# State space stage of a hybrid decoder: where tap loads queue, how many projection banks, how far apart the groups

## The chip, the cores and the metric

The kernel runs on one core of one Trainium2 chip. The metric is the device time of one execution in microseconds; the median of three runs of the kernel before is 1704.26 us. Engine names are those of the profile: PE is TensorE's matrix multiply and PEld its weight load, DVE is VectorE, ACT is ScalarE, POOL is GpSimd, SP is the engine that issues all DMAs here.

## The reference, cut

Two layers on a (1024, 1024) float32 sequence. Layer 0 is dilated attention. Layer 1, where the change lies, is a state space layer:

```python
def s5_mixer(h, w_in, ..., w_glu, b_glu, w_out):
    proj = h @ w_in                                   # 1024 x 2048
    u, z = proj[..., :SSM_WIDTH], proj[..., SSM_WIDTH:]
    y = s5_scan(u, ...)        # 64 groups of 16 channels, 64 complex states each
    g = jax.nn.gelu(y)
    y = g * jax.nn.sigmoid(g @ w_glu + b_glu)
    return (y * jax.nn.silu(z)) @ w_out

# in s5_scan, per group:
#   states_t = a_bar * states_(t-1) + b_bar u_t ;  y_t = Re(C states_t) + d u_t
```

Both layers are wrapped in RMS norms and a residual addition. Float32 products are made on TensorE from a high and a low part of each operand, three matmuls per product (high·high, high·low, low·high).

## The kernel before, in words

The sequence is cut in halves of 512 tokens. A *half projection* is 24 matmuls (8 slices of the inner dimension, three products each) of one 128-column block `e` of the weight with one token half `th`, into one bank of PSUM. The input projection of layer 1 has 16 blocks, so 32 halves, counted t = 0 to 31: blocks 0 to 7 give u, 8 to 15 give z. `in_order` emits them; `proj_half` takes the bank from the pool `psj`, which has two. `use_u` copies a bank with ScalarE (L1389) and stores it to DRAM (`u_dr`, L1391); `use_z` forms silu with ScalarE (L1396) and VectorE (L1397) and stores it (`z_dr`, L1398). A bank is free for the next half when its last reader is through. Each block's weight is loaded (L95), split in high (`whi`, ScalarE, L83) and low part (`wlo`, VectorE, L84).

The scan is cut in eight groups of SSM heads, one object `Ssm` each, with five stages:

- `ssm_loads`: tables from DRAM: BT, Cg, Sg, and CA (576 KB), two buffers each.
- `ssm_taps`: eight DMAs of 64 KB bring the short convolution M ("taps"). Taps of groups 0 to 3 share one large tile (tag `b1`), those of 4 to 7 another (`b3`).
- `ssm_input`: reads the group's u back in another layout, as U (512 KB), two buffers.
- `ssm_states`: matmuls pv = BT·U (L1339), rotation by Cg and Sg and scans on VectorE, two multiplies or additions on GpSimd, result X (L1352).
- `ssm_outputs`: matmuls py = M·U + CA·X (L1366, L1367), GELU over ScalarE, GpSimd and VectorE (L1368 to L1373), store to `y_dr` (L1374).

`layer1` writes down after which half t each stage of each group is emitted: group e begins at 3e, its loads at +3 (earlier for groups 0 and 1), taps at +4, U at +5, states at +7, outputs at +10. That order is a priority. The final order on each engine is found at build time by a scheduler that plays the program through with a cost model and takes, on each engine, the first instruction in priority that is ready at that moment of its model; `high_priority` moves work ahead by 600 places. On the chip each engine then works through its list strictly in order, waiting on semaphores. `tc.issue_after(x)` puts what is traced in its block behind `x` in the list of `x`'s engine, with no wait for `x` to finish.

After the stage comes `glu`: it reads y back (`gy`, L1431), splits it in high and low part (g0 in the tiles `b1` and `b3`, which held the taps; g1 in `b4`, `b5`), and starts with four half projections at once in two `psj` and two `psl` banks (`psb`), seven of the eight inner slices first, the eighth at the end.

PSUM has eight banks in four pools of two here: `psj` (projections), `pst` (transposes, of the norm before the stage), `pso` (py) and `psl` (pv).

Of the kernel before, what the change touches and what calls it, by code (L numbers as in the profile page):

```python
# [15 lines left out]
F32 = mybir.dt.float32  # L16
# [7 lines left out]
P = 128  # L24
# [3 lines left out]
H = 512  # L28
# [61 lines left out]
def load_w(c, src):  # L90

    nc = c.nc
    with c.tc.high_priority(AHEAD):
        raw = c.wraw.tile([P, KT * P], F32, tag="wraw", name="wraw")
        nc.sync.dma_start(raw, src)  # L95
        hi = c.wsp.tile([P, KT * P], F32R, tag="whi", name="whi")
        lo = c.wsp.tile([P, KT * P], F32R, tag="wlo", name="wlo")
        c.last_lo = split(c, hi, lo, raw, engine=c.w_engine).ins
    return hi, lo


def proj_part(c, ps, w, h, ks, first=True):

    nc = c.nc
    wh, wl = w
    hh, hl = h
    for k in ks:
        s = slice(k * P, k * P + P)
        for n, (a, b) in enumerate(((wh, hh), (wh, hl), (wl, hh))):
            nc.tensor.matmul(ps, a[:, s], b[:, k, :], start=first and k == 0 and n == 0,  # L110
                             stop=k == KT - 1 and n == 2, skip_group_check=True)


def proj_half(c, w, h):

    ps = c.psj.tile([P, H], F32, tag="psj", name="psj")
    proj_part(c, ps, w, h, range(KT))
    return ps

# [629 lines left out]
def in_order(c, srcs, h, use, after=None, start=None, ws=()):  # L749

    t = 0

    def one(e, th, ps):
        nonlocal t
        use(e, th, ps)
        if after:
            after(t)
        t += 1  # L760

    ws = list(ws) or [load_w(c, srcs[e]) for e in range(2 if start else 0)]
    if start == "block":
        jobs = [(e, th) + ((c.psj, "psj"), (c.psl, "psl"))[th] for th in range(2) for e in range(2)]
        pss = [pool.tile([P, H], F32, tag=tag, name="psb") for _, _, pool, tag in jobs]
        for ks in (range(KT - 1), (KT - 1,)):
            for ps, (e, th, _, _) in zip(pss, jobs):
                proj_part(c, ps, ws[e], h[th], ks)
                if ks[0]:
                    one(e, th, ps)  # L770
    elif start == "half":
        for e in range(2):
            one(e, 0, proj_half(c, ws[e], h[0]))
        pss = [c.psj.tile([P, H], F32, tag="psj", name="psj") for _ in range(2)]
        for part in range(2):
            cs = slice(part * 256, part * 256 + 256)
            for e in range(2):
                proj_part(c, pss[e][:, cs], ws[e], [x[:, :, cs] for x in h[1]], range(KT), part == 0)
                if part:
                    one(e, 1, pss[e])  # L780
    for e in range(len(ws), len(srcs)):
        w = load_w(c, srcs[e])
        for th in range(2):
            one(e, th, proj_half(c, w, h[th]))


def silu2(c, t, ps):
# [7 lines left out]
def attn_gate(c, a, h):  # L795

    nc = c.nc
    g = [(c.pb.tile([P, KT, H], F32R, tag=f"b{i}", name=f"gh{i}"),
          c.pb.tile([P, KT, H], F32R, tag=f"b{2 + i}", name=f"gl{i}")) for i in range(2)]
    raw = [c.pb.tile([P, KT, H], F32, tag=f"b{4 + i}", name=f"wo{i}") for i in range(2)]  # L800

    def load_out(p, n):
        nc.sync.dma_start(raw[n][:, p, :], a["w_out"][p, :, n * H:n * H + H])

    def early(p):
        load_out(p, 0)
        for i in range(2):
            if p == 7:
                f = c.last[:, i * H:i * H + H]
            else:  # L810
                f = c.slot("fz")
                nc.sync.dma_start(f, c.on_dr[p, :, i * H:i * H + H])
            split(c, g[i][0][:, p, :], g[i][1][:, p, :], f)

    def use(p, th, ps):
        if th == 0:
            load_out(p, 0)
        t = c.slot("tz")
        silu2(c, t, ps)
        f = c.slot("fz").rearrange("p (i n) -> p i n", i=8)  # L820
        nc.sync.dma_start(f, c.on_dr[p].rearrange("p (i n) -> p i n", i=8)[:, :, 64 * th:64 * th + 64])
        nc.gpsimd.tensor_tensor(f, f, t.rearrange("p (n i) -> p i n", i=8), op=ALU.mult)
        for i in range(2):
            dh, dl = (x[:, p, :].rearrange("p (i n) -> p i n", i=4)[:, :, 64 * th:64 * th + 64] for x in g[i])
            split(c, dh, dl, f[:, 4 * i:4 * i + 4, :])

    def step(t):
        if t < 7 - EARLY:
            early(EARLY + t)

    in_order(c, [a["w_in"][48 + p] for p in range(EARLY)], h, use, step)
    run_merge(c)
    early(7)
    for p in range(8):
        load_out(p, 1)
    return g, raw
# [453 lines left out]
def ssm_loads(self):  # L1290

    c, et = self.c, self.et
    nc = c.nc

    def tl(name, w=128):
        return c.ssm.tile([P, 8, w], F32, name=name, tag=name, bufs=2)

    self.BT, self.Cg, self.Sg = tl("BT"), tl("Cg"), tl("Sg")
    self.CA = tl("CA", 144)
    dr = c.rot_dr  # L1300
    nc.sync.dma_start(self.BT, c.bt_dr[et].rearrange("p (g x) -> p g x", g=8))
    for hf in HEADS:
        nc.sync.dma_start(self.Cg[hf].rearrange("p g x -> p (g x)"),
                          bass.AP(dr.tensor, dr.offset + et * 3 * 64 * S, [[S, 64], [1, S]]))
    nc.sync.dma_start(self.Sg.rearrange("p g x -> p (g x)"),
                      bass.AP(dr.tensor, dr.offset + (et * 3 + 1) * 64 * S, [[S, P], [1, S]]))
    nc.sync.dma_start(self.CA, c.ca_dr[et].rearrange("p (g x) -> p g x", g=8))


def ssm_taps(self):  # L1310

    c, et = self.c, self.et
    if et % 4 == 0:
        c.taps.append(c.pb.tile([P, 4, 8, P], F32, tag=("b1", "b3")[et // 4], name="taps"))
    t = self.M = c.taps[et // 4][:, et % 4]
    for m in range(8):
        src = bass.AP(c.k_dr.tensor, c.k_dr.offset + et * 8 * 16 * 240 + 16 * m, [[240, 16], [16 * 240, 8], [1, 128]])
        c.nc.sync.dma_start(t[16 * m:16 * m + 16], src)


def ssm_input(self):
    c = self.c
    self.U = c.ssm.tile([P, 8, P], F32, name="U", tag="U", bufs=2)
    c.nc.sync.dma_start(self.U, c.u_dr[self.et].rearrange("p (g n) -> p g n", g=8))


def ssm_states(self):
# [54 lines left out]
def layer1(c, a, h1, ws):  # L1382

    nc, tc = c.nc, c.tc
    c.ssm = c.es_pa.enter_context(tc.tile_pool(name="ssm", bufs=1, side="left", reuse_waits="tile"))
    def use_u(et, th, ps):
        ut = c.slot("ut")
        with tc.high_priority(AHEAD):
            nc.scalar.copy(ut.rearrange("p (i n) -> p i n", i=4)[:, ::-1, :], ps.rearrange("p (i n) -> p i n", i=4))  # L1389
            dst = bass.AP(c.u_dr.tensor, c.u_dr.offset + et * P * S + (1 - th) * 4 * 16384, [[P, P], [16384, 4], [1, P]])  # L1390
            nc.sync.dma_start(dst, ut.rearrange("p (i n) -> p i n", i=4))  # L1391

    def use_z(et, th, ps):
        z = c.slot("z1")
        with tc.high_priority(AHEAD):
            nc.scalar.activation(z, ps, AF.Tanh, scale=0.5)  # L1396
            nc.vector.scalar_tensor_tensor(z, z, 1.0, ps, op0=ALU.add, op1=ALU.mult)  # L1397
            nc.sync.dma_start(c.z_dr[et, :, th * H:th * H + H], z)  # L1398

    groups = [Ssm(c, a, e) for e in range(8)]  # L1400
    c.taps = []
    at = [[] for _ in range(40)]
    for e in range(8):
        t = 3 * e
        for stage, d in ((ssm_loads, (-1, -2)[e] if e < 2 else 3), (ssm_taps, 4), (ssm_input, 5), (ssm_states, 7), (ssm_outputs, 10)):
            at[t + d + 1].append((stage, e))

    def run(t):
        for stage, e in at[t + 1]:
            stage(groups[e])  # L1410

    def use(e, th, ps):
        (use_u if e < 8 else use_z)(e % 8, th, ps)

    run(-1)
    in_order(c, [a["ssm_w_in"][e] for e in range(16)], h1, use, run, start="half", ws=ws)
    for t in range(32, 39):
        run(t)
# [32 lines left out]
def trunk(tc, a):  # L1451
    c = Ctx()
    nc = tc.nc
    c.nc, c.tc = nc, tc
    c.turn = 0
    with ExitStack() as es:
        pool = lambda name, **k: es.enter_context(tc.tile_pool(name=name, **k))
        c.cst = pool("cst", bufs=1)
# [45 lines left out]
        g, raw = attn_gate(c, a, h)  # L1504
# [112 lines left out]
```

## Time and profile before

| | |
|---|---|
| median of three runs (lowest to highest) | 1704.26 us (1700.07 to 1706.83) |
| the profiled execution's own time | 1699.39 us |
| its span, first to last instruction | 1697.6 us |
| busy in the span: PE, DVE, ACT, POOL | 98%, 60%, 42%, 27% |
| first projection matmul of layer 1 | 1261.33 us |
| last output matmul of group 7 | about 1501.8 us |
| first matmul after the four starting banks of the GLU | 1532.87 us |
| DMA share from 1261.33 to 1501.77 | 0.68, at 202 GB/s |

The profile is one execution. A row of the timeline gives start, duration, engine, line, operation, tiles (written <- read), shape and count, and in brackets how long the engine had been idle and what released it. A row of a window gives start and end, length, busy time and count by engine, the granted TensorE clock (1.00 is full), the DMA engines' mean busy share and their GB/s. Matmuls are pipelined: one of 512 columns is shown with 0.40 us, and the next starts 0.23 us after it.

### The profile page before, as it was taken

To read this page: it belongs to the slowest core of one execution; us is meant where nothing else is said; L and a number is where in the kernel's file an instruction comes from. 1 tells how busy PE (TensorE), PEld (TensorE's weight loads), DVE (VectorE), ACT (ScalarE), POOL (GpSimd) and SP (SyncE) were. 2 spreads that over 40 slices of the span, in tenths; PEclk is the share of its full clock that TensorE was granted. 3 is DMA by queue.
4 is the path that set the end of the run, shared out by engine and by line. 5 is a ranking of instruction groups with operands and counts; after the bars stand their busy time and mean duration, and the time that the engine had idled before them with its cause. 6 is when DMAs were issued, how large, how long until landed. Compare 5 with 4: busy or idle time off the path is not lost. (4 is left out here: it accounts for less than half of the span.)

```text
span 1697.6 us, 26292 instructions
## 1 busy us (share of the span) xinstructions
PE 1657.5 (98%) x9714; PEld 1397.0 (82%) x9714; DVE 1014.2 (60%) x2509; ACT 711.9 (42%) x1730; POOL 461.0 (27%) x303
## 2 busy tenths in 40 slices
PE   8999999999999999999999999999999999989998
PEld 6889999978888888888888888877887888867886
DVE  8698898625554554545454554657562787755533
ACT  5232232236465464655555454653452223233411
POOL 2000001132242525223351614213220445413121
PEclk9999999999999999999999999999999999989999
DMA  6223455532331423232242424236259865465432
GB/s 236 84 55 101 147 175 162 174 95 65 87 106 54 117 70 103 78 91 90 77 117 82 113 68 124 78 110 167 87 169 237 232 203 202 143 186 162 149 118 87
DMA packets 176857, 212.19 MB, mean 125 GB/s; under 512 B 37443, under 2 KB 133462, under 8 KB 176728
## 3 DMA queue, kind: packets, MB, share of 16 engines
q1 hardware_dynamic: 176728, 210.52, 41.5%
q8 instruction: 76, 1.25, 0.3%
q14 instruction: 53, 0.43, 0.1%
HBM read 153.51 MB, written 56.96 MB: 124 GB/s over the span
## 5 line engine op out<-in xcount | busy, mean ns | idle before, releaser
L110 PE MATMUL psj<-hh,whi 128*128 128x512 f32 x896 | 359.6, 401 | 3.7 <-DVE tz L792 3.7
L110 PE MATMUL psj<-hh,wlo 128*128 128x512 f32 x896 | 359.4, 401 | 0.0
L110 PE MATMUL psj<-hl,whi 128*128 128x512 f32 x896 | 356.4, 398 | 0.0
L84 POOL TENSOR_TENSOR wlo<-wraw,whi 128x1024 fp32r<-128x1024 f32 x48 | 115.2, 2400 | 395.4 <-ACT whi L83 365.1
L110 PEld LDWEIGHTS psj<-hh,whi 128*128 128x128 f32 x896 | 169.6, 189 | 41.2 <-DVE tz L792 4.1
L110 PEld LDWEIGHTS psj<-hh,wlo 128*128 128x128 f32 x896 | 169.4, 189 | 36.6
L110 PEld LDWEIGHTS psj<-hl,whi 128*128 128x128 f32 x896 | 169.4, 189 | 36.4
L486 ACT ACTIVATE lg<-lg,nm 128x128 f32<-128x128 f32 (+1 forms) x384 | 168.2, 442 | 37.4 <-DVE nm L481 37.4
L83 ACT CAST whi<-wraw 128x1024 fp32r<-128x1024 f32 x80 | 83.7, 1046 | 192.5 <-PE psj L110 127.1
L475 DVE CUSTOM_DVE_ANT_0 lg<-psl,T 128x128 f32<-128x128 f32 (+1 forms) x384 | 110.6, 347 | 88.6 <-PE psl L469 88.6
L371 PE MATMUL psq<-whi,v 128*128 128x256 f32 x640 | 120.3, 284 | 0.0
L110 PE MATMUL psj<-h1h,whi 128*128 128x512 f32 (+1 forms) x272 | 106.7, 393 | 8.0 <-DVE z L1397 7.8
L84 DVE TENSOR_TENSOR ph<-pt,ph 128x512 fp32r<-128x512 f32 (+2 forms) x160 | 96.8, 622 | 15.3 <-ACT ph L83 13.1
L110 PE MATMUL psj<-h1l,whi 128*128 128x512 f32 (+1 forms) x272 | 105.7, 389 | 0.1
L110 PE MATMUL psj<-h1h,wlo 128*128 128x512 f32 (+1 forms) x272 | 105.2, 388 | 0.0
L84 DVE TENSOR_TENSOR kl<-psj,kh 128x512 fp32r<-128x512 f32 x48 | 33.2, 692 | 119.8 <-ACT kh L83 119.2
L371 PEld LDWEIGHTS psq<-whi,v 128*128 128x128 f32 x640 | 100.0, 189 | 1.2 <-issue 1.2
L83 ACT CAST ph<-pt 128x512 fp32r<-128x512 f32 (+2 forms) x160 | 81.5, 529 | 46.5 <-PE pt L497 45.5
L371 PE MATMUL psq<-wlo,v 128*128 128x256 f32 x320 | 91.3, 286 | 0.5 <-DVE wlo L84 0.5
L546 PE MATMUL pso<-ph,vs 128*128 128x256 f32 (+1 forms) x544 | 86.7, 284 | 0.0
L497 PE MATMUL pt<-identr,lg 128*128 128x128 f32 x560 | 82.2, 277 | 0.0
L1213 POOL TENSOR_TENSOR Ks<-Ks,O 128x16 f32<-128x16 f32 x8 | 4.3, 534 | 284.4 <-ACT Ks L1211 284.4
(283 smaller groups left out, 3696.8 us busy)
## 6 DMA issues: line engine op xcount, KB each, us to landing
wraw<-in_w_in_dram SPq DMA_DIRECT2D x56, 512.0 KB
mw<-wt_dr SPq DMA_DIRECT2D x48, 256.0 KB
v<-in_w_v_dram SPq DMA_DIRECT2D x20, 512.0 KB
vp<-v_dr SPq DMA_DIRECT2D x16, 512.0 KB
wraw<-in_ssm_w_in_dram SPq DMA_DIRECT2D x16, 512.0 KB
v_dr<-v SPq DMA_DIRECT2D x30, 256.0 KB
rot_dr<-rt SPq DMA_DIRECT2D x48, 128.0 KB
ca_dr<-ca SPq DMA_DIRECT2D x32, 144.0 KB
```

Of the source, the lines that this page charges most:

```text
L83: nc.scalar.copy(hi, src)
L84: return (engine or nc.vector).tensor_tensor(lo, src, f32(hi), op=ALU.subtract)
L110: nc.tensor.matmul(ps, a[:, s], b[:, k, :], start=first and k == 0 and n == 0, stop=k == KT - 1 and n == 2, skip_group_check=True)
L371: nc.tensor.matmul(o, r[x][:, k, ts], w[y][:, k, :], skip_group_check=True, start=i in (0, 4, 5) and t % 2 == k == n == 0, stop=k == 3 and ...
L475: nc.vector.tensor_tensor_reduce(lg[:, h, j, 0:w], psl[:, h, o], bt[:, h, 256 - w:256], scale=1.0, scalar=-3.0e38, op0=ALU.add, op1=ALU.ma ...
L486: nc.scalar.activation(lg[:, h, j, 0:w], lg[:, h, j, 0:w], AF.Exp, bias=nm[:, h, b:b + 1], accum_out=ms[:, col:col + 1])
L497: c.nc.tensor.transpose(pt[:, n * P:(n + 1) * P], lg[:, h, j, part * P:part * P + P], c.ident)
L546: nc.tensor.matmul(o, l, r, start=n == 0, stop=n == len(jobs) - 1, skip_group_check=True)
L1213: nc.gpsimd.tensor_tensor(Ks[:, 0:16], Ks[:, 0:16], self.dd, op=ALU.add)
```

## The change

- `proj_half` takes its bank in turn from `psj` and `pst` after the opening of the stage (`c.wide`), so that projections have four banks instead of two. In the rest of the kernel `c.wide` is 0.
- CA moves from `ssm_loads` to the end of `ssm_taps`. Taps and CA of a group are issued behind the load of that group's U; `ssm_taps` moves from +4 to +6, behind `ssm_input`.
- U has three buffers.
- Group e begins at (11e + 2) // 4, that is at 0, 3, 6, 8, 11, 14, 17, 19 instead of 0, 3, 6, 9, 12, 15, 18, 21.
- The tables of group 1 are issued behind the load of U of group 0 (emitted at half 5 instead of half 1).

```diff
 def proj_half(c, w, h):
-    ps = c.psj.tile([P, H], F32, tag="psj", name="psj")
+    pool, tag = ((c.psj, "psj"), (c.pst, "pst"))[c.banks % 2]
+    c.banks += c.wide
+    ps = pool.tile([P, H], F32, tag=tag, name="psj")
     proj_part(c, ps, w, h, range(KT))
...
 def in_order(...):
+    c.wide = 1 if start == "half" else c.wide
     for e in range(len(ws), len(srcs)):
         w = load_w(c, srcs[e])
         for th in range(2):
             one(e, th, proj_half(c, w, h[th]))
+    c.banks = c.wide = 0
...
 def ssm_loads(self):
-    self.CA = tl("CA", 144)
...
-    nc.sync.dma_start(self.CA, c.ca_dr[et].rearrange("p (g x) -> p g x", g=8))
...
 def ssm_taps(self):
-    for m in range(8):
-        src = bass.AP(...)
-        c.nc.sync.dma_start(t[16 * m:16 * m + 16], src)
+    self.CA = c.ssm.tile([P, 8, 144], F32, name="CA", tag="CA", bufs=2)
+    with c.tc.issue_after(self.load_U.ins):
+        for m in range(8):
+            src = bass.AP(...)
+            c.nc.sync.dma_start(t[16 * m:16 * m + 16], src)
+        c.nc.sync.dma_start(self.CA, c.ca_dr[et].rearrange("p (g x) -> p g x", g=8))
...
 def ssm_input(self):
-    self.U = c.ssm.tile([P, 8, P], F32, name="U", tag="U", bufs=2)
-    c.nc.sync.dma_start(self.U, ...)
+    self.U = c.ssm.tile([P, 8, P], F32, name="U", tag="U", bufs=3)
+    self.load_U = c.nc.sync.dma_start(self.U, ...)
...
 def layer1(...):
     for e in range(8):
-        t = 3 * e
-        for stage, d in ((ssm_loads, (-1, -2)[e] if e < 2 else 3), (ssm_taps, 4), (ssm_input, 5), (ssm_states, 7), (ssm_outputs, 10)):
+        t = (11 * e + 2) // 4
+        for stage, d in ((ssm_loads, (-1, 2)[e] if e < 2 else 3), (ssm_input, 5), (ssm_taps, 6), (ssm_states, 7), (ssm_outputs, 10)):
             at[t + d + 1].append((stage, e))

     def run(t):
         for stage, e in at[t + 1]:
-            stage(groups[e])
+            if stage is ssm_loads and e == 1:
+                with tc.issue_after(groups[0].load_U.ins):
+                    stage(groups[e])
+            else:
+                stage(groups[e])
```

More of the change, by code (lines that the diff above doesn't have):

```diff
@@ L1315, in ssm_taps @@
     t = self.M = c.taps[et // 4][:, et % 4]
-    for m in range(8):
-        src = bass.AP(c.k_dr.tensor, c.k_dr.offset + et * 8 * 16 * 240 + 16 * m, [[240, 16], [16 * 240, 8], [1, 128]])
-        c.nc.sync.dma_start(t[16 * m:16 * m + 16], src)
+    self.CA = c.ssm.tile([P, 8, 144], F32, name="CA", tag="CA", bufs=2)
+    with c.tc.issue_after(self.load_U.ins):
+        for m in range(8):
+            src = bass.AP(c.k_dr.tensor, c.k_dr.offset + et * 8 * 16 * 240 + 16 * m, [[240, 16], [16 * 240, 8], [1, 128]])
+            c.nc.sync.dma_start(t[16 * m:16 * m + 16], src)
+        c.nc.sync.dma_start(self.CA, c.ca_dr[et].rearrange("p (g x) -> p g x", g=8))
 def ssm_input(self):
     c = self.c
-    self.U = c.ssm.tile([P, 8, P], F32, name="U", tag="U", bufs=2)
-    c.nc.sync.dma_start(self.U, c.u_dr[self.et].rearrange("p (g n) -> p g n", g=8))
+    self.U = c.ssm.tile([P, 8, P], F32, name="U", tag="U", bufs=3)
+    self.load_U = c.nc.sync.dma_start(self.U, c.u_dr[self.et].rearrange("p (g n) -> p g n", g=8))
 def ssm_states(self):
@@ L1455, in trunk @@
     c.turn = 0
+    c.banks, c.wide = 0, 0
     with ExitStack() as es:
```

## The prediction

> **What bounds the kernel now.** I read the page first, then TensorE's waits in the stretch that the change touches, then time-ordered rows around each wait, then windows for rates and clock. All windows are microseconds from the start of the span.
>
> ```profile
> PE 1657.5 (98%) x9714; PEld 1397.0 (82%) x9714; DVE 1014.2 (60%) x2509; ACT 711.9 (42%) x1730; POOL 461.0 (27%) x303
> ```
>
> TensorE has work in 98% of the span, so only two things can shorten it: idle stretches of TensorE, and stretches in which its clock is cut. The state space stage runs from the first projection matmul (1261.33) to the last output matmul of group 7 (1501.77); the gated linear unit (GLU) then opens with 96 matmuls into four banks, until 1532.87. The waits of TensorE in these two stretches (total, times, longest), and the stretches themselves (length, busy time and count of each engine, granted clock, DMA share, GB/s):
>
> ```profile
> PE psj L110 <- DVE z L1397: 7.8, 3, 3.6
> PE psb L110 <- ACT g0b L83: 3.5, 2, 2.4
> PE pv L1339 <- DMA U<-u_dr: 2.6, 1, 2.6
> ...
> 1261.33:1501.77 240.44, 229.72 (x1218) 194.26 (x1216) 160.42 (x246) 66.88 (x108) 82.75 (x78) 0.99 0.68 202
> 1502.00:1532.87 30.87, 26.50 (x97) 19.69 (x95) 17.33 (x24) 14.51 (x25) 7.63 (x6) 0.89 0.69 201
> ```
>
> So three causes: TensorE waits for VectorE to empty a projection bank (L1397), for an input U of a group, and, at the GLU's start, for the split of g. Where they stand, in TensorE's order of time (start, duration, instruction, count, idle before and its releaser):
>
> ```profile
> 1303.23 0.40 PE L110 MATMUL psj<-h1h,wlo 128*128 128x512 f32 x1
> 1306.25 0.49 PE L1339 MATMUL pv<-U,BT 128*128 128x128 f32 x2 [2.62 <-DMA U<-u_dr]
> ...
> 1397.41 0.50 PE L110 MATMUL psj<-h1h,whi 128*128 128x512 f32 x1 [2.06 <-DVE z L1397]
> ...
> 1491.46 0.59 PE L110 MATMUL psj<-h1h,whi 128*128 128x512 f32 x1 [3.62 <-DVE z L1397]
> ...
> 1501.77 1.71 PE L110 MATMUL psb<-g0b,whi 128*128 128x512 f32 x3
> ...
> 1519.27 1.22 PE L110 MATMUL psb<-g0b,whi 128*128 128x512 f32 x2 [2.40 <-ACT g0b L83]
> ...
> 1532.87 0.73 PE L110 MATMUL psj<-g0b,whi 128*128 128x512 f32 x2 [0.67 <-ACT whi L83]
> ```
>
> The wait costs more than itself. Two halves of 24 matmuls (one right after the U wait, one after the 3.62 us wait) against one in an undisturbed place, projection matmuls alone:
>
> ```profile
> 1306.49:1313.72 7.23, 7.23 (x24) 5.54 (x24) 0.00 (x0) 0.00 (x0) 0.76 0.88 168
> 1491.46:1498.72 7.26, 7.26 (x24) 5.59 (x24) 0.68 (x1) 0.00 (x0) 0.76 0.85 253
> 1397.41:1403.13 5.72, 5.71 (x24) 4.44 (x24) 0.68 (x1) 0.00 (x0) 1.00 0.79 243
> ```
>
> The granted clock is 0.76 there and the half takes 7.23 and 7.26 us instead of 5.72: 1.5 us more, each time. The 2.06 us wait left the clock at 1.00.
>
> **The change, part by part.** *Loads of taps and CA behind U (SP's queue).* No DMA is added or removed: 64 tap loads, 8 CA, 8 U. Their order changes. Before, the queue of SP (start, duration, count) and one ACT row show why U is late:
>
> ```profile
> 1285.85 1.06 ACT L1389 COPY ut<-psj 128x512 f32<-128x512 f32 x2
> ...
> 1291.29 5.42 SPq L1318 DMA_DIRECT2D taps<-k_dr  x11
> 1296.96 0.93 SPq L1391 DMA_DIRECT2D u_dr<-ut  x2
> ...
> 1300.76 0.98 SPq L1324 DMA_DIRECT2D U<-u_dr  x2
> ```
>
> The copies of u were done at 1286.9, but their stores were issued at 1296.96, behind tap loads, about 0.49 us of issue each (5.42 / 11), and U was read only at 1300.76. With every tap load (and the loads of group 1) behind U of group 0, the stores go out at once and U can be asked for some 8 to 10 us sooner; its first use then comes before no wait. I take the whole 2.6 us and the 1.5 us of cut clock: 4.1. What the moved loads cost: taps and CA of group 0 and the loads of group 1 (0.5, 0.6 and 1.5 MB) now start near 1292 and are due at group 0's outputs, three halves and a group after 1308, near 1327; 2.6 MB at the stage's mean 202 GB/s are 13 us of 35. Hidden, with other traffic beside it. The bounds are 0 and what a late weight would cost (a rival below). Later groups: taps are due four halves (22 us) after their U is asked for.
>
> *Four banks.* From half 4 on, projections alternate between two psj banks and two pst banks (pst last served the transposes, done at 1279). The wait it removes, on VectorE's side:
>
> ```profile
> 1393.38 0.60 ACT L1396 ACTIVATE z<-psj 128x512 f32<-128x512 f32 x1 [4.31 <-PE psj L110]
> ...
> 1395.54 1.23 DVE L84 TENSOR_TENSOR wlo<-wraw,whi 128x1024 fp32r<-128x1024 f32 x1 [0.20 <-DVE T L1351]
> 1396.68 0.68 DVE L1397 SCALAR_TENSOR_TENSOR z<-z,psj 128x512 f32<-128x512 f32 x1
> ```
>
> ScalarE had read the bank at 1394.0, VectorE got to z at 1396.68, behind the group's rotations and a weight split, and the next projection began at 1397.41. With two more banks VectorE may be two halves (11.4 us) later before TensorE feels it. All three waits go: 7.8, and 1.5 of cut clock. Together 9.3. No instruction is added; z's own ring of buffers is unchanged.
>
> *Three U buffers.* With the new spacing U of group 3 is asked for after half 13, the very half after which group 1 has its outputs and would free the buffer; with a third buffer it need not wait. Its cost is room only.
>
> *Groups every 2.75 halves.* Group 7 begins after half 19 instead of 21, so its outputs come after half 29 instead of 31, and two halves (11.4 us) of projections lie behind them. That bears on the GLU's start, where rows of three engines show the tail (VectorE's six g splits could not begin before taps of groups 4 to 7 were read for the last time, since both live in the same memory):
>
> ```profile
> 1502.23 5.20 DVE L84 TENSOR_TENSOR g0b<-gy,g0b 128x512 fp32r<-128x512 f32 x6
> ...
> 1511.49 0.33 SPq L1374 DMA_DIRECT2D y_dr<-Y  x1
> 1515.71 5.46 SPq L1431 DMA_DIRECT2D gy<-y_dr  x5
> ...
> 1518.60 0.62 ACT L83 CAST g0b<-gy 128x512 fp32r<-128x512 f32 x1 [5.89 <-DMA gy<-y_dr]
> ```
>
> The chain from group 7's last output to its g takes 1518.6 + 1.2 − 1501.8, about 18 us. Now 11.4 us of projections and the first 84 of the 96 GLU matmuls (84 × 0.237 = 20 us) cover it. The 96 took 31.1 us from 1501.77 to 1532.87; at 5.7 / 24 us each they need 22.8. Of the 8.3 us I take 7: the 0.67 wait for a weight at the end stays, since its buffer is freed only by these matmuls.
>
> *What is late next.* VectorE and the groups' own chain. From group 2's pv to group 7's, five groups, and a group's chain in the z half (pv read, X done), beside TensorE's three blocks:
>
> ```profile
> 1359.03:1475.30 116.27, 112.11 (x602) 94.97 (x601) 92.99 (x131) 32.52 (x53) 53.00 (x51) 1.00 0.59 194
> ...
> 1376.59 0.38 PE L1366 MATMUL py<-U,taps 128*128 128x128 f32 x2
> 1380.15 1.95 PE L1339 MATMUL pv<-U,BT 128*128 128x128 f32 x16
> 1381.86 0.48 PE L110 MATMUL psj<-h1h,whi 128*128 128x512 f32 x1
> ...
> 1381.25 0.69 DVE L1340 TENSOR_TENSOR T<-Cg,pv 128x512 f32<-128x512 f32 x1 [3.15 <-PE pv L1339]
> ...
> 1397.28 1.28 DVE L1352 TENSOR_TENSOR X<-X,T 128x508 f32<-128x508 f32 x2
> ```
>
> VectorE does 92.99 / 5 = 18.6 us a group. TensorE needs 2.75 × 5.7 + 3.56 (py) + 1.71 (pv) = 20.9 us a group, so VectorE is at 89% against 80% (92.99 / 116.27) now: still not the bound, but the two short gaps of two halves (16.7 us) are under 18.6. And X was ready 17.3 us after pv (1381.25 to 1398.56), where three halves give 17.1. An output matmul may therefore wait for X in the five groups 3 to 7. The trace shows no such wait. Bounds: 0 each (the order then puts another half in between) and the 2.06 us of the bank wait each, 10.3 in all. I take 0.8 each, 4 us, nearer the lower end, because X of the first half of a group is ready sooner.
>
> **Sum**: 4.1 + 9.3 + 7 − 4 = 16.4 us off. With the ends of the unknown part, nothing and 10.3 in place of the 4, and 1.3 more at the GLU, it lies between 10.1 and 21.7. The profiled execution took 1699.39 us (span 1697.6), 4.9 under the median 1704.26 of the three timed runs. Against it the sum gives 1683.0, against the median 1687.9; the next kernel's runs will scatter in the same way, so I forecast 1686, between the two.
>
> **The rivals.** *The last groups slip* (1694). If X is late in each z group and the order puts a half in front of each output, group 7's outputs come after half 31 as now. The stage's 13.4 us stay, less some 3 of waits, the GLU's 7 do not come: 1704.3 − 10.4 = 1694. For it: 17.3 against 17.1 us above, and the short gaps. Against it: VectorE has 2.3 us a group to spare (20.9 − 18.6) to catch up.
>
> *VectorE becomes the bound* (up to 1707). The multiply of the rotation that reads two operands from on-chip memory varies (min/median/max of 16), and GpSimd's multiply beside it shows with what:
>
> ```profile
> L1351 DVE TENSOR_TENSOR T<-Sg,T x16: 684/1171/1682, 1323.1 to 1488.7; 64x512 f32<-64x512 f32 x16
> ...
> 1391.64 1.72 POOL L1348 TENSOR_TENSOR X<-Cg,T 128x508 f32<-128x508 f32 x1 [1.01 <-DVE T L1346]
> 1392.24 1.66 DVE L1351 TENSOR_TENSOR T<-Sg,T 64x512 f32<-64x512 f32 x1
> ```
>
> The 1.66 us one began inside GpSimd's 1.72. GpSimd is busy 53.00 / 5 = 10.6 us a group, which will fall into 20.9 us instead of 23.3, so more of the eight such operations of a group (L1350, L1351, L1352 and L1373, twice) can meet it. At 1.0 us each (1682 − 684) for the seven not already hit, a group takes 25.6 us, 4.7 over TensorE's 20.9; in the five groups from 3 on that is 23.5 us, more than the 20.4 gained: 1707. It decides from 2.3 us a group on. Against it: the mean over five groups holds such meetings already, and VectorE's and GpSimd's order within a group does not change. [...]
>
> *Taps late at every group* (slower, 1716). The nine loads of a group sit behind its U in a queue that goes in order. From asking for U to CA's landing I estimate 9 × 0.49 us of issue and 1.1 MB at 202 GB/s, together 10 us, against 22 us until the outputs. From 22 us on, each further microsecond is paid eight times; at 26 us it is 32 us, so 1704.3 − 20.4 + 32 = 1716. For it: from 1306 to 1313 the DMA engines were 0.88 busy while they moved only 168 GB/s, so the taps' small packets are dear, and they now come when weights, U, tables and stores all want the engines. Against it: the stage as a whole is at 0.68 and no byte is added; the loads that now wait were those that crowded 1261 to 1306.
>
> *It does not do what it says* (1704). The order on SP is fixed at build time, and the banks might be freed by the same late VectorE. But an order behind U is an order, and three half projections of slack stand where there was one.
>
> [...]
>
> **How the numbers follow.** The forecast 0.61; the last groups slip 0.18; VectorE bound 0.09; taps late 0.08; nothing happens 0.04. A measurement of this kernel can tell about 0.5% (8.5 us) from no change, so faster means under 1695.8. That holds the forecast, and most of the slip case (0.14): 0.75. Within 0.5%: 0.04 of the slip case, VectorE bound, nothing: 0.17. Slower: 0.08. The range 1676 to 1700: below by 4.9 for the scatter of runs under the lower end of the sum against the median (1704.3 − 21.7 = 1682.6) with 1.7 to spare; above over the slip case and half of the VectorE one. It leaves out about 0.17. The forecast's own range is 1678 to 1693.
>
> **What would show each step.** Right: no wait of pv for U, and stores of u issued within 2 us of their copies; no wait of psj or pst matmuls for L1397; the stage's TensorE clock at 1.00 throughout; the last py before the last two halves; the 96 GLU matmuls in under 25 us. Wrong: waits of py (L1366, L1367) for X L1352, for taps or CA; weights cast late (whi waiting for wraw, with TensorE waiting behind); VectorE above 19.5 us a group; py of group 7 again directly ahead of psb; clock cuts in the new places.

## The result, and the profile after

The changed kernel takes 1692.66 us (median of five runs, 1690.53 to 1694.92), the kernel before 1704.25 us (1700.07 to 1706.83): a ratio of 0.9932, 95% interval 0.9919 to 0.9944, or 11.6 us less. The profiled execution took 1692.66 us with a span of 1690.9. The forecast was 1686 in a range of 1676 to 1700. Ratios leave out executions at a lower clock; there is one in all that follows, of `gyo_before` (2011.59 us at a granted clock of 0.75, which its median includes).

The largest waits of TensorE in the state space stage and in the opening of the GLU, 1255 to 1545 us of the changed kernel (waiting line and its releaser: total, times, longest):

```profile
PE py L1372 <- DVE X L1357: 3.1, 1, 3.1
PE psb L110 <- ACT whi L83: 1.7, 1, 1.7
PE psb L110 <- ACT g0b L83: 1.4, 2, 1.2
PE py L1372 <- POOL Y L1376: 1.1, 1, 1.1
...
```

The wait for U and all waits for z (now L1402) are gone. Two waits of py came, in the blocks of groups 4 and 7, and the GLU's matmuls (psb) still wait. Next, windows of the changed kernel: the stage from its first projection to the first GLU matmul, the opening of the GLU, eight microseconds of that opening, and the py block of group 4 (length, busy time and count by engine, granted clock, DMA share, GB/s):

```profile
1261.90:1493.82 231.92, 227.40 (x1218) 193.05 (x1216) 163.84 (x247) 67.04 (x110) 85.34 (x82) 0.99 0.72 209
1493.82:1525.37 31.55, 27.55 (x97) 19.91 (x97) 15.57 (x23) 14.27 (x23) 3.15 (x3) 0.84 0.71 210
...
1496.97:1505.00 8.03, 6.16 (x12) 3.63 (x13) 5.86 (x8) 4.04 (x7) 0.00 (x0) 0.50 0.93 279
...
1411.37:1419.91 8.54, 5.43 (x34) 5.24 (x33) 6.13 (x9) 2.59 (x4) 0.59 (x2) 0.80 0.91 260
```

Stage and opening together take 263.5 us. Before they took 271.5 (1261.33 to 1532.87), so 8.1 us of the gain lie here, and they lie in the stage: 231.9 against 240.4. The opening kept its length (31.55 us; 1501.77 to 1532.87 was 31.1). The profiled spans differ by 6.7 us (1697.6 and 1690.9) where the medians differ by 11.6: the profiled execution before was 4.9 us under its median.

The chain of SyncE around U of group 0, the changed kernel (start, duration, instruction, count):

```profile
1287.01 0.36 SPq L1396 DMA_DIRECT2D u_dr<-ut  x1
...
1288.45 0.36 SPq L1396 DMA_DIRECT2D u_dr<-ut  x1
1289.35 0.33 SPq L1329 DMA_DIRECT2D U<-u_dr  x1
...
1309.48 1.95 PE L1344 MATMUL pv<-U,BT 128*128 128x128 f32 x16
```

U is asked for at 1289.35 instead of 1300.76, 20 us ahead of pv, which starts with no wait.

The last group did move: its py block (1477.37, with the wait of 1.1) ends at 1482.14, and two half projections lie between it and the GLU. Yet the opening is as long as before, and it is still matmuls that wait for g0, g1 and a weight that set it (start, duration, instruction, count, idle before and its releaser):

```profile
1496.97 1.22 PE L110 MATMUL psb<-g0b,whi 128*128 128x512 f32 x2 [1.69 <-ACT whi L83]
1499.67 1.22 PE L110 MATMUL psb<-g1b,whi 128*128 128x512 f32 x2 [0.65 <-ACT g1b L83]
1502.08 1.22 PE L110 MATMUL psb<-g0b,whi 128*128 128x512 f32 x2 [1.18 <-ACT g0b L83]
```

### The profile page after: what moved, and what is told of

The parts are those of the page before. It is cut to its first block, busy times and chain, and to the rows that moved or that the text cites. A ratio compares the mean times of both kernels' runs of the same rounds, so it can differ in the third digit from the quotient of the medians.

```text
span 1690.9 us, 26326 instructions
## 1 busy us (share of the span) xinstructions
PE 1654.9 (98%) x9714; PEld 1394.5 (82%) x9714; DVE 1016.6 (60%) x2509; ACT 711.9 (42%) x1730; POOL 456.1 (27%) x303
## 3 DMA queue, kind: packets, MB, share of 16 engines
q8 instruction: 76, 1.25, 0.3%
## 4 chain that ended last, share of the span: by engine, by line
PE 89%; DVE 5%; DMA 4%; issue 1%; SPq 1%; ACT 0%; POOL 0%; DVEq 0%; ACTq 0%; POOLq 0%
PE psj L110 47%; PE psq L373 11%; PE psl L471 5%; PE pso L548 4%; PE pt L499 4%; PE pso L852 4%; PE pso L851 3%; PE pso L850 3%; PE psb L110 1%; PE pso L574 1%; PE psv L234 1%; PE psv L232 1%; PE psv L233 1%; PE pst L127 1%; DVE T L1351 1%
```

## The experiments

Times are medians, and each ratio is against the kernel before, run beside it. "Opening" is the time from the first GLU matmul to the first matmul after the 96.

| run | us (ratio) | 95% interval | opening, us |
|---|---|---|---|
| changed kernel | 1692.66 (0.9932) | 0.9919 to 0.9944 | 31.6 |
| `banks` | 1690.68 (0.9930) | 0.9914 to 0.9945 | 34.4 |
| `order` | 1696.52 (0.9962) | 0.9948 to 0.9977 | 29.9 |
| `sp3` | 1689.26 (0.9920) | 0.9904 to 0.9937 | 33.6 |
| `gyo` | 1691.99 (0.9941) | 0.9921 to 0.9960 | 24.5 |
| `y1o` | 1686.57 (0.9901) | 0.9883 to 0.9918 | 31.6 |
| `gyo_y1o` | 1679.37 (0.9851) | 0.9828 to 0.9874 | 23.5 |
| `sp3_gyo` | 1677.52 (0.9845) | 0.9827 to 0.9862 | 23.4 |
| `sp3f_gyo` | 1680.40 (0.9863) | 0.9844 to 0.9881 | 23.0 |
| `space` | 1702.83 (1.0005) | 0.9993 to 1.0017 | 31.3 |
| `nobanks` | 1698.55 (0.9980) | 0.9969 to 0.9992 | 30.2 |
| `gyo_before` | 1698.65 (0.9977) | 0.9966 to 0.9989 | 24.0 |
| `banks_gyo` | 1678.98 (0.9875) | 0.9860 to 0.9889 | 23.4 |

**`banks`: the kernel before with four banks alone.**

```diff
-    ps = c.psj.tile([P, H], F32, tag="psj", name="psj")
+    pool, tag = ((c.psj, "psj"), (c.pst, "pst"))[c.banks % 2]
+    c.banks += c.wide
```

> The kernel before with the four projection banks and nothing else of the change. If the waits for L1397 were a matter of banks, all three go (7.8 us, and the half speed half behind the longest, 1.5): 1704.3 becomes about 1695, the U wait of 2.6 stays, and the GLU's 96 opening matmuls keep their 31 us. If VectorE was the bound behind the banks, the waits come back in another place (an output matmul waiting for X, or a half later the same wait) and the time stays above 1700.

1690.68 us, 12.4 less than the kernel before beside it. In the traces the stage is 12.4 us shorter (228.0, from 1261.97 to 1489.99) and the opening 3.3 longer. Its largest waits of TensorE, 1255 to 1545 us:

```profile
PE psb L110 <- DVE g0b L84: 2.8, 2, 2.2
PE psb L110 <- ACT whi L83: 2.3, 1, 2.3
PE psj L110 <- ACT whi L83: 2.3, 2, 1.6
PE psb L110 <- ACT g0b L83: 0.8, 2, 0.5
...
```

The timeline has pv of group 0 at:

```profile
1311.44 2.05 PE L1343 MATMUL pv<-U,BT 128*128 128x128 f32 x16
```

The z waits are gone, and so is the wait of pv for U, though no load was moved. The reason is in the order: pv now stands behind eight full halves (it starts at 1311.44), where it stood behind seven before (1306.25, after its wait). That with two banks the eighth half had no free bank at that point of the build-time order, and pv was put ahead of it for that reason, is inferred; that four banks move pv by one half and end the wait is shown. The U wait had two sufficient cures.

**`order`: the order of the loads alone** (two banks, two U buffers, a group every three halves).

```diff
-    c.banks += c.wide
+    c.banks += 0
...
-    self.U = c.ssm.tile([P, 8, P], F32, name="U", tag="U", bufs=3)
+    self.U = c.ssm.tile([P, 8, P], F32, name="U", tag="U", bufs=2)
...
-        t = (11 * e + 2) // 4
+        t = 3 * e
```

> The kernel before with the order of loads alone: taps and CA behind U, the tables of group 1 behind U of group 0; groups every 3 halves, two banks, two U buffers. If the crowd of tap loads made U late, the U wait (2.6) and the half speed half behind it (1.5) go, and 1704.3 becomes about 1700. If the moved loads come late somewhere else (a weight, a store of y, tables), the gain is eaten and new waits stand in the z halves: 1702 to 1708.

1696.52 us, 6.5 less; in the traces the stage is 4.2 us shorter (236.3), which is the 4.1 of the prediction, and the opening 1.2 shorter. No wait for U, with pv still behind seven halves; the z waits, in the waits of TensorE, stay as they were:

```profile
PE psj L110 <- DVE z L1402: 7.7, 3, 3.6
```

**`sp3`: the whole change, but a group every three halves.**

```diff
-        t = (11 * e + 2) // 4
+        t = 3 * e
```

> The changed kernel with groups every 3 halves instead of 2.75; all else as changed. Theory: the wait of group 4's outputs for X (3 us and half speed behind it, 8.5 us for a block of 3.6) comes from the gap of two halves between groups 2 and 3; at 3 halves it goes, and the GLU's opening matmuls do not care, since they wait for reads of y that are queued behind the last two z: 1692.7 becomes about 1687. Rival: group 7's outputs behind the last half make the GLU wait for y longer, as forecast, and 2.75 is worth its wait: 1693 to 1699.

1689.26 us, 13.8 less. There is no wait of py left, and stage and opening take 259.8 us (1263.45 to 1523.22). The intervals of this run and of the changed kernel overlap, so the times alone don't rank the two; the traces show 263.5 against 259.8 us and the two py waits in one only. The 2.75 spacing costs the stage 5.7 us there (231.9 against 226.2) and shortens the opening by 2.0 (31.6 against 33.6). That `banks` (12.4) and `order` (6.5) sum to more than 13.8 fits the shared cure of the U wait.

**`gyo`: the changed kernel with buffers of its own for gy.** If the opening waits for group 7's data, this changes nothing; if it waits for the buffers that gy is read into, the opening shortens. The buffers are four tiles of a pool that lies idle in the stage, two reads to a tile, instead of the ring of seven slots (tags a and b, taken in turn) that z also uses.

```diff
-            y = c.slot("gy")
+            if et % 2 == 0:
+                yo = c.outs.tile([P, D], F32, tag="O", name="gy", bufs=4)
+            y = yo[:, et % 2 * H:et % 2 * H + H]
```

> The changed kernel with the reads of y for the GLU (gy) in buffers of their own (four tiles of two reads each, in a pool that is idle then) instead of the ring that they share with z. Theory: the GLU's gain did not come because gy, in the ring, gets its buffers behind z of halves 30 and 31 and its even blocks before its odd ones; with own buffers the 96 opening matmuls take 23 to 25 us instead of 31.5, and 1692.7 becomes about 1686. Rival 1: the splits on VectorE and ScalarE or the DMA rate are the bound: under 2 us are gained. Rival 2: early reads crowd VectorE's and ScalarE's queues in the z halves, and waits for X grow: 1693 or more.

The opening fell by 7.0, to 24.5 us at a full clock. The groups of gy's reads, first of the changed kernel, then of `gyo` (count: min/median/max ns, first and last start):

```profile
L1440 SPq DMA_DIRECT2D gy<-y_dr x16: 359/366/547, 1489.9 to 1512.8; - x16
```

```profile
L1442 SPq DMA_DIRECT2D gy<-y_dr x16: 359/371/565, 1343.6 to 1505.1; - x16
```

and the window of `gyo`'s opening:

```profile
1497.42:1521.93 24.51, 22.90 (x97) 17.83 (x95) 11.16 (x18) 9.12 (x15) 2.58 (x2) 1.00 0.69 215
```

In the changed kernel not one of the 16 reads starts before 1489.9; the first of `gyo`, at 1343.6, shows how early the first groups lie in DRAM. And the last seven start after the last z store, long after the store of group 7 (1486.66); SyncE's rows of the changed kernel (start, duration, instruction, count):

```profile
1486.66 2.86 SPq L1379 DMA_DIRECT2D y_dr<-Y  x2
1489.87 1.53 SPq L1440 DMA_DIRECT2D gy<-y_dr  x3
1491.45 0.50 SPq L1403 DMA_DIRECT2D z_dr<-z  x1
1494.52 3.97 SPq L1440 DMA_DIRECT2D gy<-y_dr  x6
1499.11 0.43 SPq L1403 DMA_DIRECT2D z_dr<-z  x1
1499.64 0.52 SPq L1440 DMA_DIRECT2D gy<-y_dr  x1
...
1502.78 10.36 SPq L1440 DMA_DIRECT2D gy<-y_dr  x6
```

and the waits of SyncE's queue from 1486 to 1515 us (total, times, longest):

```profile
SPq L1440 <- DVE g0b L84: 7.2, 6, 1.4
SPq L1379 <- DVE Y L1378: 5.5, 2, 3.4
...
SPq L1440 <- DMA z_dr<-z: 1.0, 1, 1.0
```

The reads wait for the split of an earlier gy and for the store of a z, that is for a slot of the ring. In SyncE's list as built they also stand behind the two stores of group 7's y, for which SyncE waited 5.5 us: three reads ahead of the store of z of half 30, six between it and that of half 31 (blocks 1 and 3 of the first token half behind the even ones), the other seven behind both. With buffers of their own, 13 of the 16 reads stand ahead of these stores, six of them far up in the stage. The buffers decide both the waits for slots on the chip and the order that the scheduler finds, for reads and for matmuls; the run does not separate the two.

The time is 1691.99 us all the same, for the two py waits and their cut clocks grew (0.69 from 1411 to 1422; blocks of groups 4 and 7: 9.90 and 7.43 us, where an undisturbed one takes 3.57 and the changed kernel had 8.54 and 4.77); TensorE's waits in `gyo`:

```profile
PE py L1372 <- DVE X L1357: 3.2, 1, 3.2
PE py L1372 <- POOL Y L1376: 2.1, 1, 2.1
```

So 7 us were won in the opening and 3.7 of them paid in the stage (235.6 against 231.9). The rest of the loss is not in this trace, whose execution took 1688.47 us, the shortest of the six. What made the py blocks longer here wasn't isolated.

**`y1o`: the changed kernel with more buffers for y (Y1).** Its theory: the wait of py for X of group 4 comes from the output of group 3, which has no buffer to be written to, because group 2's stores are late. Y1 had two buffers (`bufs=2`), not the four of the expectation below.

```diff
-        T1, T2 = (c.ssm.tile([P, 4, P], F32, name=n, tag=n, bufs=2) for n in ("Y1", "Y2"))
+        if b == 0:
+            yo = c.outs.tile([P, D], F32, tag="O", name="Y1", bufs=4)
+        T1 = yo[:, b * H:b * H + H].rearrange("p (g x) -> p g x", g=4)
+        T2 = c.ssm.tile([P, 4, P], F32, name="Y2", tag="Y2", bufs=2)
```

> The changed kernel with eight buffers for Y1 (the GELU's half of py, stored to y_dr) instead of four in two steps of two: pairs in four tiles of an idle pool. Theory: group 4's outputs wait for X because ScalarE sits 5.2 us before Y of group 3 until a store of y gives its buffer back, VectorE's list has Y of group 3 ahead of group 4's scans and stands idle for 3.8 us, and X is 3 us late. With more buffers the block of group 4's outputs takes 3.6 us instead of 8.5: 1692.7 becomes about 1688. Rival: VectorE is late by its own work in the gap of two halves (17 to 18 us of work in 16.7), so the block still takes over 6 us and the time stays within 2 us of 1692.7.

1686.57 us, 17.0 less than before; py of group 4 is back at 3.57 us. The wait of 1.1 us in group 7's block stays, so that one has another cause. The chain in the timeline of the changed kernel, engine by engine (SyncE, ScalarE, VectorE, TensorE):

```profile
1389.69 0.38 SPq L1379 DMA_DIRECT2D y_dr<-Y  x1
1392.11 1.70 SPq L1322 DMA_DIRECT2D taps<-k_dr  x3
1394.46 0.34 SPq L1379 DMA_DIRECT2D y_dr<-Y  x1
...
1395.99 0.60 ACT L1373 ACTIVATE Y<-py 128x512 f32<-128x512 f32 x1 [5.22 <-DVE T L1347]
...
1398.33 0.60 ACT L1373 ACTIVATE Y<-py 128x512 f32<-128x512 f32 x1 [1.25 <-DMA y_dr<-Y]
...
1399.96 0.69 DVE L1378 SCALAR_TENSOR_TENSOR Y<-Y,Y 128x512 f32<-128x512 f32 x1 [1.94 <-ACT Y L1377]
1402.50 1.11 DVE L1378 SCALAR_TENSOR_TENSOR Y<-Y,Y 128x512 f32<-128x512 f32 x1 [1.85 <-ACT Y L1377]
1403.54 4.79 DVE L1351 TENSOR_TENSOR_SCAN T<-rho,T 128x128 f32<-128x128 f32 x8
...
1414.13 1.28 DVE L1357 TENSOR_TENSOR X<-X,T 128x508 f32<-128x508 f32 x2
...
1411.37 0.38 PE L1371 MATMUL py<-U,taps 128*128 128x128 f32 x2
1414.86 0.80 PE L1372 MATMUL py<-X,CA 128*128 128x128 f32 x2 [3.11 <-DVE X L1357]
```

The y stores of group 2 are issued with tap loads between them, while the DMA engines are 0.90 busy (1386 to 1398). ScalarE stands 5.22 us before it can write group 3's first Y, and 1.25 us before the second. VectorE, which has group 3's Y ahead of group 4's scan in its list, stands 1.94 and 1.85 us. X of group 4 comes 3.1 us late for TensorE. The row of 5.22 names VectorE's T as the releaser, a wait for several things put down to the last; that the buffer is the cause is shown by the run: with eight Y1 buffers, and Y of group 3 still ahead of group 4's scan on VectorE, the same ScalarE row, in the timeline of `y1o`, follows its matmul within 0.36 us.

```profile
1395.23 0.60 ACT L1376 ACTIVATE Y<-py 128x512 f32<-128x512 f32 x1 [0.36 <-PE py L1375]
```

**`gyo_y1o`: both edits.**

> Own buffers for gy and more for Y1 in the changed kernel, both from the same idle pool. Theory: the GLU's opening stays at 24.5 us as with gy alone, and the waits for X (9.9 and 7.4 us blocks there instead of 3.6 each) go: about 10 us under the kernel with gy alone, 1682. Rival: the waits for X come from VectorE's work, not from Y1: within 3 us of the kernel with gy alone, 1689 to 1695.

1679.37 us, 24.2 less: 7.2 below `y1o`, run beside it. py of group 4 takes 3.57 us, of group 7 4.79, and the opening 23.5.

**`sp3_gyo`: gy's own buffers, a group every three halves** (the edits of `sp3` and `gyo`). Here group 7's outputs are directly ahead of the GLU, as in the kernel before.

> Groups every 3 halves as in the kernel with that alone, and own buffers for gy. Here group 7's outputs come behind the last half again. If the forecast of the tail holds once gy is free, the GLU's opening waits for the low parts of g (their memory is taken by taps until the last output) and for group 7's y: 27 to 30 us instead of 33.6, total about 1684. If gy's ring was the whole of it, the opening takes 24 to 25 us: about 1680.

1677.52 us, 26.0 less, the lowest median (its interval overlaps with those of `gyo_y1o` and `sp3f_gyo`). Only one wait of TensorE is left in 1255 to 1545 us, and the stage and the opening run at a full clock:

```profile
PE psj L110 <- ACT whi L83: 0.3, 1, 0.3
```

The windows of the stage (without its first 0.3 us) and of the opening:

```profile
1263.45:1488.46 225.01, 224.86 (x1216) 191.19 (x1215) 160.09 (x246) 70.02 (x114) 78.55 (x77) 1.00 0.76 221
1488.46:1511.86 23.40, 23.00 (x99) 17.75 (x97) 16.03 (x20) 9.88 (x17) 8.39 (x6) 1.00 0.73 222
```

The last py of group 7 starts at 1488.32 and the first GLU matmul at 1488.46, yet the opening is 23.4 us. With buffers of its own for gy, group 7's tail is not the opening's bound.

**`sp3f_gyo`: the same with every stage of a group two halves earlier.**

```diff
-        for stage, d in ((ssm_loads, (-1, 2)[e] if e < 2 else 3), (ssm_input, 5), (ssm_taps, 6), (ssm_states, 7), (ssm_outputs, 10)):
+        for stage, d in ((ssm_loads, (-1, 0)[e] if e < 2 else 2), (ssm_input, 3), (ssm_taps, 4), (ssm_states, 5), (ssm_outputs, 8)):
```

> Groups every 3 halves, own buffers for gy, and every stage of every group two halves earlier (U after half 3, states after half 5, outputs after half 8), so that group 7's outputs lie two halves before the end, as with 2.75, but with no short gap. Theory: no wait for X, a GLU opening of about 24.5 us: 224.6 us of stage and 24.5 of opening, about 1679. Rival: U of group 0 and the tables come too late for a start two halves earlier (U is asked for at 1289, first used at about 1297), and the tap loads crowd weights: a wait of 3 to 6 us in the first 60 us of the stage, 1683 to 1687.

1680.40 us, and an interval that overlaps with that of `sp3_gyo`: no gain from an earlier group 7 can be told.

**`space`: the kernel before with the 2.75 spacing and three U buffers alone.**

```diff
-    self.U = c.ssm.tile([P, 8, P], F32, name="U", tag="U", bufs=2)
+    self.U = c.ssm.tile([P, 8, P], F32, name="U", tag="U", bufs=3)
...
-        t = 3 * e
+        t = (11 * e + 2) // 4
```

> The kernel before with groups every 2.75 halves and three U buffers alone: two banks, loads as before. Since 2.75 made the full change dearer than 3 (1692.7 against 1689.3), it should not help alone: the three waits for L1397 stay or move, the short gap brings a wait for X, and the GLU's opening keeps over 30 us because of gy's ring: 1702 to 1710. Rival, the forecast's own step: group 7 two halves sooner shortens the GLU's opening by 7 us by itself: about 1697.

1702.83 us, a ratio of 1.0005: no gain, and an opening of 31.3 us. The expected wait for X did not come.

**`nobanks`: the changed kernel with two banks** (`c.banks += 0`).

> The changed kernel with two projection banks instead of four. The order of loads alone gave 6.5 us, so if banks and spacing are independent of it, this is the order's gain less the price of the spacing: 1697 to 1702, with the waits for L1397 back. If the short gaps and two banks hurt each other, 1703 or more.

1698.55 us. The z waits are back, and longer than before (7.8), by TensorE's waits:

```profile
PE psj L110 <- DVE z L1402: 10.7, 3, 5.6
```

**`gyo_before`: the kernel before with gy's own buffers alone.**

> The kernel before with own buffers for gy alone. If the ring was the whole of the GLU's wait, the 96 opening matmuls take 24 us instead of 31.1 here too, and 1703.5 becomes about 1696. If the tail of group 7 was the cause, as forecast (its outputs are the last thing before the GLU), about 30 us stay and the time does not move: over 1701.

1698.65 us, 3.6 less, where about 1696 was expected. The opening fell by 7.1 us, to 24.0, though group 7's outputs are still directly ahead of it, but TensorE's old waits grew from 7.8 and 2.6:

```profile
PE psj L110 <- DVE z L1397: 9.5, 4, 3.6
PE pv L1339 <- DMA U<-u_dr: 3.6, 1, 3.6
```

**`banks_gyo`: the kernel before with four banks and gy's own buffers.**

> The kernel before with four banks and own buffers for gy, no new order of loads. With four banks alone the U wait was gone, because the half that had lacked a bank now stands ahead of pv, and a wait for a weight of 2.3 us had come. If the order of loads is worth only that weight, this is about 2 to 3 us above the kernel with order, banks and gy (1677.5): about 1680. If the tap loads cost more than that without the new order, 1684 or more.

1678.98 us, 23.2 less, with one wait of 0.3 us left in the stage and an opening of 23.4. Four banks, and own buffers for gy, which are no part of the change, do nearly all that any of these kernels gained; `sp3_gyo`, with the order of the loads (and a third U buffer) added, has 0.9845 against 0.9875 here, with intervals that just touch.

## Why the prediction was right or wrong

**Loads of taps behind U (4.1): the effect is right, the cause was incomplete.** The wait went, as `order` shows alone, with a stage 4.2 us shorter. But the sum gave this edit a gain that the banks alone bring too, through pv's place in the order. In the full change the two terms are not separate.

**Four banks (9.3): right in the stage, but with a cost put at nothing.** `banks` removes every z wait and, with the wait for U, 12.4 us of the stage, where both terms together were forecast at 13.4. But it lengthens the opening of the GLU by 3.3 us (34.4 against 31.1), which the sum does not have. Taking the banks out of the change (`nobanks`) brings the z waits back and costs 5.9 us between the medians (1698.55 against 1692.66), about 8 by the ratios (0.9980 against 0.9932).

**The opening of the GLU (7): wrong, and this is the step that failed.** The prediction read 18 us from group 7's last output to its g, took that chain for the bound, and had it covered by two halves of projections and the first 84 of the 96 matmuls. The chain was there: in the kernel before, the read at 1515.71 waited 3.8 us for group 7's y, and TensorE then 2.40 us for its g. The waits of SyncE's queue there, 1488 to 1535 us:

```profile
SPq L1431 <- DMA z_dr<-z: 7.4, 2, 5.2
...
SPq L1431 <- DMA y_dr<-Y: 3.8, 1, 3.8
```

But only 48 matmuls, not 84, stood ahead of that wait (it ended 17.5 us after the first one, where 84 take 20), and other reads had waited 7.4 us for stores of z, whose slots they needed. With group 7 moved, the waits for slots were left, and all reads now stood behind group 7's stores: in the changed kernel TensorE's last wait of note stands ahead of the ninth matmul (1502.08). So the size was right (7 us lie there: `gyo` 24.5, `gyo_before` 24.0, against 31.1), and the cause was the buffers of gy. In `gyo_before` group 7 is where it was, 84 matmuls do stand ahead of the first that needs its g, and they hide the chain. With two banks, moving group 7 gained nothing there (`space` 31.3 against 31.1, `nobanks` 30.2 against 29.9 of `order`); beside four banks it gained 2.0 (31.6 against 33.6 of `sp3`), less than the banks had cost. In the prediction's own rows there was a hint: behind the last store of y (1511.49) stood five reads of gy in a row (from 1515.71), and one group needs only two.

**Waits for X (−4): near in sum, wrong in shape.** It was priced as 0.8 in each of five groups. It came as one wait of 3.1 in group 4, whose block took 8.54 us instead of 3.57 (5.0 lost, with the cut clock), and one of 1.1 in group 7 (4.77): 6.2 in all. The mechanism in group 4 wasn't VectorE's load, but Y1's two buffers behind late stores (`y1o`). The wait in group 7 stayed in `y1o`, and no run isolates it. In the trace VectorE's two X there (L1357) took 2.35 us from 1476.95, where the two of group 4 took 1.28, beside GpSimd's multiply for an earlier Y (L1376, 1476.88 to 1478.16), which the wait names as its releaser: a meeting such as the rival of VectorE had priced.

**Sum.** The stage was forecast 9.4 us shorter (4.1 + 9.3 − 4) and came 8.5 shorter; the opening was forecast 7 shorter and came 0.4 longer. Together the traces show 8.1 of the 16.4, the medians 11.6. That the time lies in the range, and by 0.3 us inside the forecast's own of 1678 to 1693, is in part luck: the 3.5 us between 8.1 and 11.6 are not in these stretches of the two profiled executions, and where they lie is not shown.

**The rivals.** *The last groups slip* gave 1694, close to the time, but by a mechanism that did not occur: the last py was two halves ahead of the GLU. Its time was near because it, too, left out the GLU's 7. *VectorE as the bound* did not come. From group 2's pv to group 7's, VectorE was busy 86.10 of 101.24 us in the changed kernel, 17.2 a group, where TensorE needed 20.2:

```profile
1353.92:1455.16 101.24, 98.13 (x523) 83.66 (x521) 86.10 (x120) 28.47 (x46) 50.35 (x49) 0.98 0.77 220
```

The group of the multiply that meets GpSimd (count: min/median/max ns):

```profile
L1356 DVE TENSOR_TENSOR T<-Sg,T x16: 684/1661/1691, 1319.1 to 1474.6; 64x512 f32<-64x512 f32 x16
```

Its median rose from 1171 to 1661 ns. Ten of the 16 took 1.66 to 1.69 us, and each of the ten began inside a multiply of GpSimd (L1353 or L1376); the other six took 0.68 or 0.69 us, and none of them began inside one. In the kernel before, eight of the 16 (L1351) took 1.66 to 1.68 us. So the meetings became more, as that rival said, but only in group 7's block is a wait of TensorE put down to one. *Taps late* did not come as a wait of py for taps. Tap loads now stand between y's stores, ahead of the wait for X; how much of the stores' lateness is theirs no run isolates.

**The cut clock.** It came where the prediction asked to look, in new places: in group 4's py block after a wait of 3.11 us (0.80 in the window), and in the opening, 0.50 for the 8 us from 1496.97; in the 3.75 us before that, TensorE had started four matmuls, at 0.23 us each. In the kernel before, the half after the wait of 2.62 us ran at 0.76, that after 2.06 us at 1.00. In `gyo`, after the wait of 2.07 us in group 7's block, matmuls from 1482.66 to 1485.65 started 0.43 us apart instead of 0.23, the pace that the changed kernel's opening had at 0.50. So the length of one wait does not decide it here. In that opening, waits of 0.65 and 1.18 us broke TensorE's work until 1502.08, and the clock was back at 1.00 from 1507; what brings it back is not shown. The loss of the opening is thus waits, 4 us, and slow matmuls, about as much (31.55 − 22.8 = 8.8).

## What to carry to other kernels

When the next stage starts late, look at what its loads wait for, the buffer as well as the data: here a ring shared with the stage before held them, and moving the producer earlier was worth nothing with two banks and 2 us with four, where buffers of their own were worth 7 to 11. Two cures for one wait don't add; run each part of a change alone before summing its terms. And a tighter spacing pays only once the buffers that the groups hand on (Y1 here) are enough: with gy's own buffers, a group every 2.75 halves took 1692.0 us, and 1679.4 with more Y1 buffers as well, while one every three halves took 1677.5 without them.

## What the runs showed of the hardware

A half clock that lasts while TensorE is fed piecemeal: 0.50 from 1496.97 to 1505.00, at 77% busy by the records and with no wait over 1.2 us inside, 1.7 just before. The length of a wait alone does not tell whether the clock is cut: 2.06 us left it at 1.00 in the kernel before, and 2.07 us in `gyo` was followed by matmuls 0.43 us apart instead of 0.23. And the DMA engines' busy share does not tell what they move: 0.88 at 168 GB/s in the half after the U wait of the kernel before, beside tap loads, 0.93 at 279 in that window of the opening.
